# A hybrid decoder layer on one core: attention by pairs of heads over all tokens instead of by blocks of queries

## The chip, the cores and the metric

The kernel runs on one core of a Trainium2 chip. The metric is the device time of one execution in microseconds (us), the median of several runs; lower is better. The engines are TensorE (PE in the profile, with its weight loads as PEld), VectorE (DVE), ScalarE (ACT), GpSimd (POOL) and SyncE (SP, which here only issues DMAs). Each engine works through its own queue in order and waits on semaphores of the others.

## The reference

One layer over 512 tokens of width 1024, in float32: half a SwiGLU feed-forward (width 2816), a mixer, half a second feed-forward, each with an RMS norm before and after. The change is in the mixer alone.

```python
proj = h @ w_in          # 512 lru | 512 gate | 512 q | 128 k | 128 v
y_lru  = rg_lru(x_lru, ...) * gelu(gate_lru)
y_attn = sliding_window_sink_attention(q, k, v, sinks)   # 8 heads, 2 kv heads, dim 64
y = concat([rms_norm(y_lru, g_lru_out), rms_norm(y_attn, g_attn_out)]) @ w_o
# rg_lru: xc = conv4(x) + b;  r, i = sigmoid(block_diag(xc));  log_a = 8 r log_sigmoid(lam)
#         h_t = a h_(t-1) + sqrt(1 - a^2) i xc
# attention: a query sees itself and the 127 tokens before it, by blocks of 128:
#         p = exp(s - m) / (sum exp(s - m) + exp(sink - m));  out = p @ v
```

## The kernel before

Channels lie on partitions and the 512 tokens along the free axis, unless said otherwise. A product in full precision is three matmuls in rounded float32 (F32R): high by high, high by low and low by high (`mm3`); eight such steps of k make one product of 128 output channels. Splitting a tile into its parts is an ACT copy for the high part and a DVE subtraction for the low one. Matmuls on plain F32 tiles are used where no split exists, as in the values.

Weights pass through a class `Weights` (`W`): raw tiles of 1 MB loaded by SP into five buffers, each cut into units. `W.cast(n)` rounds the next units on ACT, `W.fill(n)` also subtracts on DVE and loads the next raw tile when one is used up, `W.take` hands a unit to PE. The order of all this is written out by hand: the program's order is each engine's queue.

The order in the mixer before:

- The boundary leaves the four lru input products (`xl_banks`) in PSUM. `conv_in` copies them to padded tiles on ACT, `conv` makes four taps (one on ACT, three on DVE).
- Products for k and v, then for the four q pairs. Product `pq{j}` holds head j of the first key-value head in rows 0 to 63 and head j of the second in rows 64 to 127. Between them `lru_gates` makes the two block-diagonal gates per 128 channels (PE, three ACT activations, one product on POOL).
- Then ten steps (`now`) over eight units (b, n): block b of 128 queries, key-value head n, four heads each. `scores` masks and takes the maximum on DVE, `exps` takes the exponential with its sum on ACT, `turn_p` transposes the four probability blocks on PE, copies them on ACT and masks them on POOL into a current and a previous part, `values` multiplies with the probabilities as stationary (128 columns) and v as moving (64 columns), and divides by the denominator at the end (`yn`). One unit is in `scores`, the one before in `turn_p`, the one before that in `values`. Block 0 uses unsplit copies (`q0`, `k0`).
- PE's filler is the four gate products (`fill_steps`, taken by `pump`, listed in `PUMPS`). The LRU's decay, root and scan and the gelu of the gates are put beside the steps by `later` and `run_due`.
- At the end the attention's rows lie with tokens on partitions and are transposed back (`atp`, 16 transposes) before they are split into high and low. `ssq` holds their sums of squares, from ACT.
- The output product `wo` takes attention channels first. After the first 36 matmuls `balance` makes the two norms, of which the LRU's comes from a PE product with a column of ones (`rms_lru`); `rescale` brings the attention half to the LRU's scale.

## Time and profile before

| | |
|---|---|
| median of 3 runs | 862.33 us (862.09 to 862.57) |
| profiled execution | 861.82 us, span 860.1 us |
| granted TensorE clock | 0.999 |
| PE busy | 850.4 us (99% of the span) |
| DVE, ACT, POOL busy | 647.5 (75%), 528.6 (61%), 168.0 us (20%) |

How to read it: the span goes from the first to the last instruction. A line of a group names the line of the kernel, the engine, the operation, the tiles (output, then inputs), the shape and the count, then the busy time in us and the mean of one in ns, then the idle time of the engine ahead of it and what ended it. In a timeline a line gives the start, the duration and the count of a run of like instructions; instructions of a full queue overlap slightly, so that a start minus the start before is less than a duration. A PE duration includes latency; what counts in a full queue is the distance between starts. In a table of stretches the numbers after the length are busy time (and count) of PE, PEld, DVE, ACT and POOL.

### The profile page before, as it was taken

The page shows a single profiled execution, that of the slowest core. Times are in us where ns is not written, and L with a number is a line of the kernel's source. Part 1 is how long each engine was busy: PE and PEld are TensorE (multiplying, and loading weights), DVE is VectorE, ACT ScalarE, POOL GpSimd, SP SyncE. Part 2 cuts the span into 40 slices and gives each one's busy share as a digit, 9 for nine tenths or more (in the row PEclk, how much of TensorE's full clock was granted, in tenths as well). Part 3 has the DMA queues.
Part 4 walks back from the last instruction along what each step waited for, and adds up shares of the span by engine and source line. Part 5 has one row for each costly group of instructions (what it writes and reads, how often), then busy time and mean ns, then how long its engine had stood idle before and what let it go on. Part 6 is the DMA issues. An engine that isn't in the chain of part 4 may idle for free.

```text
span 860.1 us, 14177 instructions
## 1 busy us (share of the span) xinstructions
PE 850.4 (99%) x5550; PEld 776.9 (90%) x5550; DVE 647.5 (75%) x883; ACT 528.6 (61%) x903; POOL 168.0 (20%) x202
## 2 busy tenths in 40 slices
PE   9999999999999999999999999999999999999996
PEld 8888999989989998998788889888998998998995
DVE  4989897887898866765688475357488788889856
ACT  6647567566576564755786677335556657658552
POOL 2022005014034011004255030001101402204402
PEclk9999999999999999999999999999999999999999
DMA  8265439739469463142112308235433945938912
GB/s 246 99 196 196 133 107 228 195 93 236 139 121 269 138 217 102 50 147 98 50 50 75 98 1 297 95 118 177 147 94 90 236 146 141 227 99 191 274 75 98
DMA packets 92867, 124.42 MB, mean 145 GB/s; under 512 B 5825, under 2 KB 62465, under 8 KB 92801
## 3 DMA queue, kind: packets, MB, share of 16 engines
q1 hardware_dynamic: 76240, 86.68, 31.8%
q0 software_dynamic: 16416, 36.71, 19.2%
q8 instruction: 43, 0.70, 0.3%
q14 instruction: 24, 0.19, 0.1%
q10 hardware_dynamic: 144, 0.13, 0.0%
HBM read 93.10 MB, written 30.41 MB: 144 GB/s over the span
## 4 chain that ended last, share of the span: by engine, by line
PE 93%; ACT 2%; DVE 2%; DMA 1%; POOL 1%; SPq 1%; issue 0%; DVEq 0%; ACTq 0%
PE aa L819 12%; PE ab L819 11%; PE da L819 6%; PE db L819 5%; PE wo L1624 4%; PE ba L819 3%; PE bb L819 3%; PE mn L701 1%; PE an L701 1%; PE yal L1146 1%; PE yal L1148 1%; PE yb L1148 1%; PE yb L1146 1%; PE yal L1147 1%; PE yb L1147 1%; PE yaa L1156 1%
## 5 line engine op out<-in xcount | busy, mean ns | idle before, releaser
L927 POOL DMA_DIRECT2D yp_a<-stage x42 | 37.0, 1160 | 146.4 <-ACT stage L924 141.2
L927 POOL DMA_DIRECT2D yp_b<-stage x42 | 36.5, 1121 | 149.0 <-ACT stage L924 142.8
L1175 POOL DMA_DIRECT2D yp_b<-stage x8 | 4.3, 541 | 91.8 <-ACT stage L1174 91.0
L1146 PE MATMUL yal<-whi_ad,hha 128*128 128x512 f32 x48 | 18.9, 393 | 0.0
L1148 PE MATMUL yal<-whi_ad,hla 128*128 128x512 f32 x48 | 18.7, 390 | 0.0
L1147 PE MATMUL yal<-wlo_ad,hha 128*128 128x512 f32 x48 | 18.7, 389 | 0.0
L1146 PE MATMUL yb<-whi_bd,hhb 128*128 128x512 f32 x48 | 18.7, 389 | 0.0
L1147 PE MATMUL yb<-wlo_bd,hhb 128*128 128x512 f32 x48 | 18.7, 389 | 0.0
L1148 PE MATMUL yb<-whi_bd,hlb 128*128 128x512 f32 x48 | 18.7, 389 | 0.0
L189 DVE TENSOR_TENSOR wlo_bd<-raw_bd,whi_bd 128x1024 fp32r<-128x1024 f32 x10 | 12.1, 1223 | 8.1 <-ACT whi_bd L184 8.1
L1297 POOL TENSOR_TENSOR xcl<-xc,xch 128x512 fp32r<-128x512 f32 x4 | 6.3, 1572 | 57.0 <-ACT xch L1296 57.0
L189 DVE TENSOR_TENSOR wlo_ad<-raw_ad,whi_ad 128x1024 fp32r<-128x1024 f32 x10 | 12.2, 1221 | 4.0 <-ACT whi_ad L184 4.0
L552 POOL TENSOR_TENSOR xg_f<-xh_f,xl_f 128x256 f32<-128x256 f32 x8 | 5.8, 767 | 43.9 <-DVE xl_f L483 43.9
L409 PE MATMUL gt<-xh_mx,whi_gt 128*128 128x512 f32 x32 | 14.2, 442 | 0.0
L602 ACT ACTIVATE sqxr<-x_rows 128x512 f32<-128x512 f32 x16 | 10.0, 631 | 5.6 <-DVE x_rows L632 5.6
L189 DVE TENSOR_TENSOR wlo_wo<-raw_wo,whi_wo 128x1024 fp32r<-128x1024 f32 x7 | 8.5, 1223 | 6.4 <-ACT whi_wo L184 6.2
L1147 PE MATMUL ybl<-wlo_bd,hhb 128*128 128x512 f32 (+1 forms) x36 | 13.2, 366 | 0.0
L1146 PE MATMUL ybl<-whi_bd,hhb 128*128 128x512 f32 (+1 forms) x36 | 13.2, 366 | 0.0
L1148 PE MATMUL ybl<-whi_bd,hlb 128*128 128x512 f32 (+1 forms) x36 | 13.2, 365 | 0.0
L1704 POOL TENSOR_TENSOR yp_b<-yp_b,grow 128x512 f32<-128x512 f32 x6 | 7.7, 1291 | 27.2 <-ACT ysq L1697 27.2
L1697 ACT ACTIVATE ysq<-yp_b 128x512 f32<-128x512 f32 (+1 forms) x9 | 5.2, 583 | 12.4 <-DVE yp_b L1696 11.7
L1624 PE MATMUL wo<-whi_wo,ylh 128*128 128x512 f32 x32 | 12.7, 396 | 0.0
(1841 smaller groups left out, 3719.9 us busy)
## 6 DMA issues: line engine op xcount, KB each, us to landing
yp_a<-stage POOLq DMA_DIRECT2D x50, 256.0 KB, 7.3
yp_b<-stage POOLq DMA_DIRECT2D x50, 256.0 KB, 7.8
raw_ad<-in_ffn_w_down SPq DMA_DIRECT2D x4, 1024.0 KB
raw_wo<-in_w_o SPq DMA_DIRECT2D x4, 1024.0 KB, 5.0
raw_bd<-in_ffn_w_down SPq DMA_DIRECT2D x4, 1024.0 KB
xn<-in_x SPq DMA_DIRECT2D x8, 256.0 KB, 3.0
x_rows<-in_x POOLq DMA_DIRECT2D x4, 512.0 KB, 12.4
yp_a<-yp_a POOLq DMA_DIRECT2D x8, 256.0 KB, 9.4
```

The costliest lines, as they stand in the source:

```text
L189: low.tensor_sub(two(lo, x), x, two(hi.bitcast(F32), x))
L409: pe.matmul(ps, hi[:, k, :], xh, start=start, stop=False)
L602: act.activation(wt(f"sq{name}{self.name}{tb}{dh}"), src, AF.Square, accum_out=self.ss[name, tb][:, dh:dh + 1])
L701: pe.matmul(b[:, l], w[part][:, k, :], xs[k][xpart][:, l], start=k + part + xpart == 0, stop=stop and k == KD - 1)
L819: pe.matmul(o, w[:, k, js], x, start=first and i + j + k == 0, stop=k == 3 and i == 2, skip_group_check=True)
L927: pool.dma_start(o, st.rearrange("p (a b) -> p a b", a=2) if len(o.shape) == 3 else st, accum_op=ALU.add)
L1146: pe.matmul(ps, hh[:, blk], hi[:, k, cs], start=start, stop=False)
L1147: pe.matmul(ps, hh[:, blk], lo[:, k, cs], start=False, stop=False)
L1148: pe.matmul(ps, hl_[:, blk], hi[:, k, cs], start=False, stop=stop)
L1156: pe.matmul(banks[i], hh[:, js], hi[:, k, :], start=first and k == 0, stop=False, skip_group_check=True)
L1624: pe.matmul(wo_banks[tb][dh], x, w[:, k, :], start=start and k == 0 and w is hi and not xp, stop=stop and k == 1 and xp == 1, skip_group_c ...
L1704: pool.tensor_mul(y, y, grow[dh][:, c0:c1])
```

## The change

Attention goes by pairs of heads j (head j of either key-value head) over all four query blocks.

- `products(j)` uses the split q and k for block 0 too and spreads the four blocks over two banks per head (block 1 and 2 in one, 0 and 3 with one key block less in the other).
- `scores(j, n)` has two more copies under the mask of 128 columns; the sink's exponential takes its bias on ACT.
- `normalise(j, n)`, new, adds the sink, takes the reciprocal and multiplies all four probability blocks on DVE, ahead of `turn_p`.
- `turn_p(j, n)` masks into tiles by key block (`pc`), with four smaller selects on POOL.
- `values(j)` has 64 columns of v as stationary and up to 256 columns of probabilities as moving; the two heads go to the two halves of the output partitions. The result has channels on partitions, so `yn` and the output transposes go. `rows_high` and `rows_low` split it and add up its squares (`acca`), whose mean is another PE product in `balance`.
- q products 1 to 3 and the gate products are the filler now, in the order q1, gt0, q2, q3, gt1 to gt3. The LRU's gates follow k, v and q0 directly; decay, root and scans 2, 3 stand ahead of pair 0's turn or behind it, scans 0 and 1 and the gelu steps in a table `beside`.
- `conv` reads the PSUM banks without padding; its split parts lie in other buffers. q3's low part is subtracted on DVE instead of POOL, and the deferred subtraction of one wo unit is gone. The wo rows of the attention half are loaded in two DMAs each, by channel order (d, j), and the gain row likewise.

```diff
+    def load_wo(k0, dh):
+        ...
+        for n in range(2):
+            sync.dma_start(raw[n * HD:(n + 1) * HD], src[n * KC * HD:(n + 1) * KC * HD].rearrange("(j d) c -> d j c", d=HD))
-    def conv(c0, xps):
+    def conv(c0):
+        for ci in (c0, c0 + 1):
+            act.activation(xcs[ci], xl_banks[ci], AF.Identity, bias=..., scale=...)
+        for back in range(1, CONV):
+            for ci in (c0, c0 + 1):
+                o = xcs[ci][:, back:]
+                dve.scalar_tensor_tensor(o, xl_banks[ci][:, :T - back], ..., o, op0=ALU.mult, op1=ALU.add)
+    def products(j):
+        ...
+        for b in range(NB):
+            i, o = ((1, 0), (0, 0), (0, 2 * P), (1, P))[b]
+            blk, keys = slice(b * P, (b + 1) * P), slice(max(b - 1, 0) * P, (b + 1) * P)
+            for p, (q_, k_) in enumerate(((qh, kh), (qh, kl), (ql, kh))):
+                for n, pr in enumerate(rows):
+                    pe.matmul(score_banks[j, n][i][:, o:o + keys.stop - keys.start], q_[pr, blk], k_[pr, keys], ...)
+    def scores(j, n):
+        ...
+        dve.copy_predicated(mid[:, 1::2, :], up8[:, :2, :], mid[:, 0::2, :])
+        dve.tensor_reduce(mx_[:, 1:3], mid[:, 1::2, :], op=ALU.max, axis=AX.X)
+        dve.copy_predicated(ends[:, 0, :], up8[:, 0, :], neg[:, :P])
+        dve.copy_predicated(ends[:, 2, :], up8[:, 0, :], ends[:, 1, :])
+        dve.tensor_reduce(mx_[:, 0::3], ends[:, 0::2, :], op=ALU.max, axis=AX.X)
+        dve.tensor_scalar(nm, mx_, -scale, nsink[:, h:h + 1], op0=ALU.mult, op1=ALU.min)
+    def normalise(j, n):
+        dve.tensor_add(den, den, es)
+        dve.reciprocal(den, den)
+        dve.tensor_mul(v4(sc), v4(sc), den.unsqueeze(2).to_broadcast([P, NB, P]))
+    def turn_p(j, n):
+        ...
+        act.copy(pa, pt)
+        for i, t in enumerate(pairs):
+            ...
+            pool.affine_select(t[:, :, 0, :], cur, ...)
+            pool.affine_select(t[:, :nb, 1, :], pre, ...)
+    def values(j):
+        o = bank(f"po{j}")
+        for b in range(NB):
+            w = P if b == NB - 1 else 2 * P
+            for n in range(2):
+                pe.matmul(o[n * HD:(n + 1) * HD, b * P:b * P + w], v[:, b * P + n * HD:b * P + (n + 1) * HD],
+                          unit[j, n][b // 2][:, 2 * (b % 2) * P:2 * (b % 2) * P + w], start=b == 0, stop=b == NB - 1, ...)
+    def rows_high(j):
+        x_high(ysp[KC + j], po[j], col("g_attn_out", j), ALL)
+        act.activation(acca, po[j], AF.Square)   # j > 0: a square of its own, added in rows_low
+    conv(0)
+    pk = in_product("pk", (), 1)
+    split_xc(0); split_xc(1)
+    W.cast(3)
+    conv(2)
+    W.fill(2)
+    kT = in_parts(pk, "kT")
+    split_xc(2); split_xc(3)
+    pv = in_product("pv", (), 2)
+    vT = taken(wt("vT"), pv)
+    lru_gates(0); lru_gates(1)
+    pq = in_product("pq0", (), 2)
+    lru_gates(2); lru_gates(3)
+    q_parts(0, pq)
+    ...                                   # v transposed back
+    pump(3)
+    products(0)
+    preload(AF.Exp)
+    ...                                   # decay_a 0-3, decay_b 0-3, preload(Sqrt), root 0-3
+    W.cast(2)
+    preload(AF.Exp)
+    for n in range(2):
+        scores(0, n); exps(0, n)
+    W.fill(2)
+    for n in range(2):
+        normalise(0, n)
+    pump(5)
+    for ci in range(KC):
+        root_u(ci)
+    SPLIT = W.taken + 3
+    beside = {0: [(scan, 0), (gelu_a, 0)], 1: [(scan, 1), (gelu_b, 0), (gelu_c, 0)], 2: [(gelu_d, 0)], 3: [(gelu_a, 1), (gelu_b, 1), (gelu_c, 1)]}
+    for j in range(KC):
+        if j:
+            values(j - 1)
+        for n in range(2):
+            if j:
+                scores(j, n); exps(j, n)
+        if j:
+            rows_high(j - 1)
+            W.fill(SPLIT + 2 * j - W.taken)
+        for n in range(2):
+            if j:
+                normalise(j, n)
+            else:
+                scan(2 + n)
+        if j == 0:
+            W.fill(SPLIT - W.taken)
+        W.cast(SPLIT + 2 * j + 1 - W.taken)
+        pump(5 if j else 8)
+        turn_p(j, 0)
+        pump(1)
+        turn_p(j, 1)
+        if j < KC - 1:
+            products(j + 1)
+        if j:
+            rows_low(j - 1)
+        W.fill(SPLIT + 2 * j + 1 - W.taken)
+        W.cast(SPLIT + 2 * j + 2 - W.taken)
+        for fn, i in beside[j]:
+            fn(i)
+        pump(4)
+    values(3)
+    ...
-    for ci, tp in enumerate(tps):
-        for b in range(NB):
-            pe.transpose(tp[:, b * P:(b + 1) * P], yns[b][:, ci * P:(ci + 1) * P], ident)
-        ...
-        ps = bank("rms_lru")
+        ps = bank("rms_mix")
+        for i, acc in enumerate((accl, acca)):
+            for b in range(NB):
+                pe.matmul(ps[:, i * NB + b:i * NB + b + 1], acc[:, b * P:(b + 1) * P], mean_c, start=True, stop=True)
```

386 lines of the change are left out of this document (140 added, 246 removed).

## The prediction

> **What bounds the kernel now.** I read the page's busy shares first, then a table of stretches, the chain that ended last, the timelines of the engines, and the groups by line with shapes kept apart.
>
> ```profile
> span 860.1 us, 14177 instructions
> PE 850.4 (99%) x5550; PEld 776.9 (90%) x5550; DVE 647.5 (75%) x883; ACT 528.6 (61%) x903; POOL 168.0 (20%) x202
> ...
> core 0: us, PE busy (x) PEld busy (x) DVE busy (x) ACT busy (x) POOL busy (x), PEclk, DMA share, GB/s
> 415.00:432.00 17.00, 16.94 (x115) 13.32 (x115) 13.01 (x27) 13.59 (x46) 6.58 (x9) 1.00 0.16 60
> 432.00:449.00 17.00, 17.00 (x139) 15.20 (x136) 14.48 (x33) 15.00 (x45) 7.64 (x12) 1.00 0.20 63
> 449.00:464.50 15.50, 15.23 (x101) 13.25 (x100) 13.70 (x19) 8.64 (x26) 13.55 (x14) 1.00 0.32 103
> ```
>
> TensorE (PE) is never idle for long, so a matmul taken away is worth its time as long as the others can follow. The mixer, which alone is changed, runs from 377.5 us (the key product) to about 464.6 us (the first output product). In the attention part (415 to 464.5) VectorE (DVE) is already busy 13.0, 14.5 and 13.7 us of 17, 17 and 15.5. That is 83%: there is little room behind PE.
>
> **The change on PE.** The chain that ended last, then PE's timeline, then groups and one line's instructions:
>
> ```profile
> 416.41 1.09 PE cur L1427 x16
> 427.49 0.84 PE po L1501 x8
> 431.74 1.63 PE sc L1438 x24
> 463.05 1.75 PE atp L1558 x16
> 464.80 8.18 PE wo L1624 x36
> 472.97 0.79 PE rms_lru L1601 x8
> ```
> ```profile
> 421.08 1.37 PE L1481 MATMUL pt<-ident,sc 128*128 128x128 f32 x4
> 426.19 0.60 PE L1481 MATMUL pt<-ident,sc 128*128 128x128 f32 x4
> 435.92 0.33 PE L1500 MATMUL po<-v,pp 128*128 128x64 f32 x2
> 437.62 0.48 PE L409 MATMUL gt<-xh_mx,whi_gt 128*128 128x512 f32 x1
> 453.23 0.98 PE L1481 MATMUL pt<-ident,sc 128*128 128x128 f32 x4
> 455.31 0.43 PE L1501 MATMUL po<-v,pa 128*128 128x64 f32 x2 [0.25 <-POOL pa L1488]
> ```
> ```profile
> L409 PE MATMUL gt<-xh_mx,whi_gt 128*128 128x512 f32 x32 | 14.2, 442 | 0.0
> L410 PE MATMUL gt<-xl_mx,whi_gt 128*128 128x512 f32 x32 | 12.5, 391 | 0.0
> L435 PE MATMUL an<-xl_mx,whi_xl 128*128 128x256 f32 x6 | 0.9, 283 | 0.0
> L469 PE MATMUL rms_x<-dg_x,ones x4: 377/378/379, 29.1 to 29.7; 128*128 128x256 f32 x4
> L1001 PE MATMUL warm<-ident 128*128 128x128 f32 x16 | 4.2, 441 | 1.4 <-POOL ident masks.py:199 1.4
> ```
>
> - *Values.* Before: two groups of 8 at 0.84, and six of 16 from 435.92 to 437.62, 1.70 each: 11.9 us. After, each pair needs per head 256+256+256+128 = 896 columns of plain f32. Plain f32 runs as two instructions (the spread of rms_x below is two products in the code, four in the row). From the durations, 391 against 283 ns says 0.42 ns a column for rounded operands plus some 0.17 us of latency; 378 ns at 256 columns says 0.81 for plain f32. So one head costs 2x896x0.81 = 1.45 us. If the two heads, in different column halves of the array, run side by side, a pair costs 1.45 plus some 0.3 for entry and exit, 1.75; one after the other 3.2. Four pairs: 7.0 or 12.8, that is -4.9 or +0.9. No row has column halves. The nearest, the row halves of the scores, overlap: 24 instructions of 256 columns in 1.63 us are 0.068 each, where one alone would need 0.107. I take -4.9.
> - By the Trainium skill (TensorE: Matmul & The Clock Gate, Part 3: Packing small matmuls) column groups run concurrently like row groups; by it this term would also be -4.9; no run shown here has it.
> - *Output transposes* go: -1.75.
> - *Scores.* One cur group (1.09) and three of 1.63 become four of 24, some smaller: +0.6.
> - *Statistic.* Sixteen one-column instructions for eight: +0.8.
> - *Returns to the products.* The first product after another kind is slower (442 against 391 ns over 32, some 0.085 for each of 20 returns by count in the timeline); about 14 remain: -0.5.
> - *PE's waits of today*: 1.37 and 0.98 against 0.60 for four transposes, and 0.25: 1.4 us. The places go: -1.4. Transposes of probabilities and values, gates and the ten input products stay in number.
>
> Sum if nothing waits anew: -4.9-1.75+0.6+0.8-0.5-1.4 = -7.2 us.
>
> **What the other queues must do.** Before, a unit's transposes came one step behind its scores, and its values two. After, one pair's scores, exponentials and division must all be through before PE may turn it (the division is now ahead of the transposes), and PE has only 56 product steps of 0.68 us (three at 0.2275, from 8.18 for 36) as filler, 16 of them ahead of the first turn.
>
> ```profile
> 375.90 2.36 DVE L189 TENSOR_TENSOR wlo_q<-raw_q,whi_q 128x1024 fp32r<-128x1024 f32 x2 [5.82 <-ACT whi_q L184]
> 397.26 0.69 DVE L1311 TENSOR_TENSOR qT0l<-pq,qT0h 128x512 fp32r<-128x512 f32 x1 [1.66 <-ACT qT0h L1310]
> 432.04 0.19 DVE L1505 RECIPROCAL rden<-den 128x8 f32<-128x8 f32 x1
> 432.33 0.69 DVE L1508 TENSOR_TENSOR yn<-po,rden 128x512 f32<-128x512 f32 x1
> 432.94 0.42 DVE L1454 COPY_PREDICATED sc<-up,sc 128x256 f32<-128x256 uint8 x1
> 433.39 0.42 DVE L1455 TENSOR_REDUCE mx<-sc 128x2 f32<-128x256 f32 x1
> ...
> 433.73 0.42 DVE L1454 COPY_PREDICATED sc<-up,sc 128x256 f32<-128x256 uint8 x1
> ...
> 434.65 0.16 DVE L1458 SCALAR_TENSOR_TENSOR nm<-mx,nsink 128x4 f32<-128x4 f32 x1
> ...
> 446.46 1.28 DVE L1404 TENSOR_TENSOR xc<-xc,th 128x512 f32<-128x512 f32 x2
> 447.66 2.73 DVE L1409 TENSOR_TENSOR_SCAN xc<-r,xc 128x512 f32<-128x512 f32 x2
> 455.49 1.59 DVE L1409 TENSOR_TENSOR_SCAN xc<-r,xc 128x512 f32<-128x512 f32 x1
> ```
> ```profile
> L1469 ACT ACTIVATE sc<-sc,nm 128x128 f32<-128x128 f32 x24 | 8.5, 371 | 0.4 <-DVE nm L1458 0.4
> L1469 ACT ACTIVATION_READ_ACCUMULATOR sc<-sc,nm 128x1 f32 x24 | 5.0, 210 | 0.0
> L387 ACT ACT_TABLE_LOAD x3 | 3.8, 1283 | 0.1
> L1393 ACT ACTIVATE r<-r,ka 128x512 f32<-128x512 f32 x4 | 3.0, 739 | 0.0
> L1395 POOL TENSOR_TENSOR m<-r 128x512 f32<-128x512 f32 x4 | 4.2, 1039 | 1.0 <-ACT r L1393 1.0
> L1488 POOL TENSOR_SCALAR_AFFINE_SELECT pa<-pa 128x512 f32<-128x512 f32 x8 | 7.3, 909 | 2.3 <-ACT pa L1483 1.9
> ```
>
> In a full queue an instruction costs its duration less about 0.08 (two scans 2.73, next at +2.64), and 0.03 more than its duration where it needs the one before.
>
> *Front (to the first turn).* Products pk and pv (48 by 0.2275) end at 388.4, as today. Two gates (12, to 391.1), pq0 (24) and two more gates follow. The low part of pq0's weights now stands on DVE behind the six taps of conv(2) and its two casts on ACT; by those queues PE waits some 0.5, and the gates end at 399.8. ACT then has six activations (0.64 each) done at 402.0. qT0's high and low part take to 403.3, where PE, after the transposes of v and three steps, asks for them at 402.3 (scores of pair 0): 0.8. ACT runs a table load with its dummy (1.3), four decays (2.6, from 403.8 to 406.3); POOL's four squares at 1.04 end at 408.7, DVE's last sum and the last root at 410.2, a cast (1.0) and a table load take to 412.3, four exponentials with their reads (0.345 the pair, and es) to 414.0, and the division (0.16+0.19+0.69 with steps, 1.02) to 415.1. PE, with products(0) and 13 steps from 403.1, is there at 413.9: 1.2, and some 0.5 at the next two places. Front: 3.0 us. It is bounded by 0 (every low part early) and by 4.5 (this chain of 12 us a tenth longer). What pays for it is the LRU work taken ahead, which before lay beside the first steps and was not waited for.
>
> *Pair 0 to pair 1.* DVE's queue from the last exponential of pair 0 (415.6) to the end of the first division of pair 1: two divisions 2.04, qT1 low 0.61, two u products 1.20, two scans 2.64, a third 1.5, three weight splits (q3, gt1, gt2; 2.36 for two) 3.45, the copy of gate 0 0.60, scores of pair 1 twice (0.45+0.34+0.20+0.31+0.45+0.12, the 128-column copies taken as 0.28) 3.74: 15.8 us, ready at 431.4. PE in that stretch: turn 0.4, products(1) 1.75, nine steps with returns 6.3, values(0) 1.75, from 416.8: 427.0. PE waits 4.4 us at the turn of pair 1, and everything behind it on PE with it. DVE is late here, not ACT: exponentials of a head group take 1.6 us, DVE's scores of one 1.87.
>
> *Later rounds.* q2's two parts stand behind the exponentials, two activations on po, a cast on ACT and the divisions on DVE, so products(2) waits about 1.5, products(3) 1.4 in the same way. Otherwise pair 1 to pair 2 is 12.8 us on DVE (two divisions 2.04, 1.3 of waiting for that cast of q2, two low parts 1.27, two splits 2.3, a scan 1.5, a gelu step 0.64, scores 3.74) and as much on PE (two turns, ten steps 7.1, the 1.5, products and values 3.5), and pair 2 to 3 is 11.9 against 12.7. POOL's 32 smaller selects have as many elements as today's 14 (7168 a partition); a pair's eight, 1792, are 3.5 of today's at 0.909, 3.2 us, and fit into the 5.5 us of steps and products before its values; if not, up to 0.5 a pair. At the end the statistic of the LRU half must be ready 36 output products (8.18) after the last gate product, where today the output transposes stand between as well (9.9); but the high and low parts of three pairs have left ACT's and DVE's queues by then (three by 0.69 on each), so I cost it at nothing, with 1 us if that is not enough. The wo load in halves adds two issues on SP, whose queue is otherwise as long as before; a raw tile comes free when q3 is split, some 10 us ahead of the cast: nothing, and 1 us if it queues. q3's split moves from POOL to DVE and is counted above. conv reads PSUM, so four ACT copies and the memsets go, off the path; the gain row by 64 channels is loaded at the start, long before its use: nothing.
>
> New waits: 3.0+4.4+1.5+1.4 = 10.3. Net -7.2+10.3 = +3.1. Walking the queues in order instead of adding gives +2.4 at the first wo product of the last token block, since some waits take in others; applied to the kernel before, the same walk ends 0.7 late. I take +2.5. The profiled run took 861.82 us (span 860.1, 1.7 around it), 0.5 below the median of 862.33: on the median, 864.8. A change under 0.2% (1.7 us) can't be told from none.
>
> **Rivals.**
> 1. *DVE keeps up* (faster). If DVE's 15.8 us between pair 0 and pair 1 were 11.4, the 4.4 would go and the 1.5 shrink with it, and about -2.8 be left: 859.5. For it: rows vary (one scan advances the queue by 1.32, another by 1.51). Against: nearly all of the 15.8 are rows above, and the sum breaks even only with 2.5 us less.
> 2. *Column halves run in turn* (slower). +5.8 on PE; two of the four pairs hide in waits, +2.9 to 3: 867.7. For it: no row shows halves by columns in plain f32.
> 3. *A cold clock* (slower). The first TensorE instructions of the trace, of 128 plain columns, took 441 ns, where 256 such columns take 378 later; if a 4 us gap brings that state back for a time like the opening's (12 of them at twice the step of 0.107, 2.6 us instead of 1.3), 1.3 to 3 us are added: 866.8. Against: the granted clock is 1.00 in every stretch, but no gap before is over 1.4 us. The Trainium skill (TensorE: Matmul & The Clock Gate, Why this matters for your kernels) says that a gap over some 3 us sends the clock to half; this trace has no such gap.
>
> **How the numbers follow.** My case 0.50 (its own range 862.8 to 867, of which 0.2 lies within 0.2%), rival 1 0.25, rival 2 0.13, rival 3 0.12. Slower 0.55, within 0.2% 0.20, faster 0.25. The range goes from deep in rival 1 (858.0) to rival 2 with more contention (869.0).
>
> **What will show it.** A wait of PE on DVE of some 4 us ahead of the second pair's transposes, with DVE busy nearly without gaps for the 16 us before; waits of 1 to 1.5 at the scores of pairs 2 and 3; values of a pair in 1.75 us (3.2 means rival 2); the granted clock after the gap (rival 3). Wrong if DVE has gaps in that stretch, or if the front's 3 us are not there.

## The result, and the profile after

The changed kernel takes 871.52 us (median of 4 runs, 869.65 to 871.97); the kernel before, run beside it, takes 862.21 us. The ratio is 1.0103 with a 95% interval from 1.0086 to 1.0121: slower by 9.3 us. The prediction said slower, but 864.8 us and at most 869.0. The profiled execution of the changed kernel was the quickest of its four, 869.65 us; its span is 7.8 us longer than that of the kernel before (860.1).

The page's busy shares, and then the waits of TensorE (PE): us in total, how often, the longest.

```profile
span 867.9 us, 14095 instructions
PE 847.4 (98%) x5502; PEld 768.3 (89%) x5502; DVE 657.3 (76%) x898; ACT 527.4 (61%) x896; POOL 173.9 (20%) x211
```
```profile
PE pt L1376 <- DVE den L1366: 6.8, 3, 4.8
PE warm L1002 <- POOL ident masks.py:199: 1.4, 1, 1.4
PE rms_mix L1579 <- DVE acc_lru L1555: 1.0, 1, 1.0
PE po L1394 <- POOL pc L1386: 0.9, 1, 0.9
...
PE pt L1376 <- ACT yah L481: 0.3, 1, 0.3
PE sc L1340 <- DVE qT2l L1316: 0.3, 1, 0.3
...
PE sc L1340 <- ACT qT2h L1315: 0.2, 1, 0.2
...
```

Apart from the warm-up (1.4, there before as well) all that is shown lies in the mixer, and they are the loss: some 10.1 us of waiting between 376 and 500 us where the kernel before had 0.25. A table of stretches shows the engines in the three stretches that the prediction quoted of before, in the longest gap, and in the 16 us behind it:

```profile
core 0: us, PE busy (x) PEld busy (x) DVE busy (x) ACT busy (x) POOL busy (x), PEclk, DMA share, GB/s
415.00:432.00 17.00, 13.48 (x78) 10.20 (x78) 16.55 (x31) 9.43 (x32) 7.45 (x8) 0.90 0.40 81
432.00:449.00 17.00, 14.22 (x95) 10.47 (x93) 14.24 (x32) 12.36 (x39) 5.05 (x8) 1.00 0.43 106
449.00:464.50 15.50, 14.92 (x92) 10.97 (x90) 14.25 (x29) 9.67 (x28) 7.63 (x14) 1.00 0.25 78
412.80:417.60 4.80, 0.00 (x0) 0.03 (x1) 4.52 (x14) 4.79 (x22) 0.00 (x0) 1.00 0.01 2
417.60:433.60 16.00, 13.83 (x78) 10.17 (x78) 15.62 (x28) 8.43 (x26) 7.45 (x8) 0.89 0.52 105
```

PE was busy in 16.94 of the first 17 us before and is now busy in 13.48; DVE went from 13.01 to 16.55. The granted clock, 1.00 in every stretch before, is 0.90 there. PE's timeline has the places:

```profile
417.60 0.72 PE L1376 MATMUL pt<-ident,sc 128*128 128x128 f32 x4 [4.80 <-DVE den L1366]
427.00 1.73 PE L1394 MATMUL po<-pc,v 128*64 128x256 f32 x14 [0.92 <-POOL pc L1386]
433.71 0.63 PE L1376 MATMUL pt<-ident,sc 128*128 128x128 f32 x4 [1.35 <-DVE den L1366]
440.75 1.73 PE L1394 MATMUL po<-pc,v 128*64 128x256 f32 x16
442.42 0.50 PE L410 MATMUL pq<-xh_mx,whi_q 128*128 128x512 f32 x1
470.06 0.39 PE L1602 MATMUL wo<-whi_wo,yah 128*128 128x512 f32 x1
479.33 1.05 PE L1579 MATMUL rms_mix<-mean_c,acc_lru 128*128 128x1 f32 x8 [0.95 <-DVE acc_lru L1555]
```

The first output product starts at 470.06 (464.56 before, +5.5 us); the wait for the statistic and its eight further instructions add 2.0 more. A pair's values, from 440.75 to the next product at 442.42, take 1.67 us, where the prediction had 1.75 for column halves side by side and 3.2 for one after the other: they do run side by side.

Where did the 7.8 us come from? Taking each row's start to the next row's start from 376 to 500 us, the waits rise by 9.9 us, and the work on PE that the change touches falls by 2.1 (at full clock by 3.9, in a later kernel without the slow rows); 9.9 - 2.1 = 7.8.

### The profile page after: what moved, and what is told of

It is laid out like the page before. It is cut to its first block, busy times and chain, and to the rows that moved or that the text cites. A ratio compares the mean times of both kernels' runs of the same rounds, so it can differ in the third digit from the quotient of the medians.

```text
span 867.9 us, 14095 instructions
## 1 busy us (share of the span) xinstructions
PE 847.4 (98%) x5502; PEld 768.3 (89%) x5502; DVE 657.3 (76%) x898; ACT 527.4 (61%) x896; POOL 173.9 (20%) x211
## 4 chain that ended last, share of the span: by engine, by line
PE 85%; DVE 7%; ACT 4%; DMA 2%; issue 1%; SPq 0%; POOL 0%; DVEq 0%; ACTq 0%
PE aa L820 12%; PE ab L820 11%; PE da L820 6%; PE db L820 5%; PE ba L820 3%; PE wo L1602 3%; PE bb L820 3%; PE an L702 1%; PE mn L702 1%; PE yal L1148 1%; PE yal L1149 1%; PE yal L1147 1%; PE yb L1149 1%; PE yb L1147 1%; PE yb L1148 1%; DMA raw_second<-in_ffn_w_gu 1%
## 5 line engine op out<-in xcount | busy, mean ns | idle before, releaser
L1385 POOL TENSOR_SCALAR_AFFINE_SELECT pc<-pa 128x256 f32<-128x256 f32 x16 | 10.8, 676 | 32.3 <-ACT pa L1378 32.3
L1268 DVE SCALAR_TENSOR_TENSOR xc<-an,cols,xc 128x511 f32<-128x511 f32 (+2 forms) x12 | 8.2, 742 | 9.0 <-ACT xc L1264 9.0
L410 PE MATMUL pq<-xh_mx,whi_q 128*128 128x512 f32 x32 | 13.6, 425 | 0.0
```

The source lines that it names most:

```text
L410: pe.matmul(ps, hi[:, k, :], xh, start=start, stop=False)
L1268: dve.scalar_tensor_tensor(o, xl_banks[ci][:, :T - back], col("conv_w", (CONV - 1 - back) * KC + ci), o, op0=ALU.mult, op1=ALU.add)
L1385: pool.affine_select(t[:, :, 0, :], cur, pattern=[[0, 2], [1, P]], base=0, channel_multiplier=-1, compare_op=ALU.is_ge, fill=0.0)
```

## The experiments

Theory at the start: the recurrence's decays, ahead of pair 0's exponentials and stretched because DVE and POOL work on SBUF at once, make the 4.8 us gap, and the gap makes half a clock behind it. Rival: DVE owes too much between 403 and 465 us, wherever one puts it. The edits are shortened: `...`, and words such as `x4` or `scores, exps of pair 0`, stand for code that isn't shown. Profiled runs reach the mixer up to 1.3 us apart, by what happens ahead of it; where that matters, times are counted from the key product. DVE's and POOL's timelines of the changed kernel, on which the theory rests:

```profile
404.79 6.12 DVE L1301 SCALAR_TENSOR_TENSOR th<-m,th 128x512 f32<-128x512 f32 x4 [1.96 <-POOL m L1298]
...
420.19 2.70 DVE L1310 TENSOR_TENSOR_SCAN xc<-r,xc 128x512 f32<-128x512 f32 x2
422.82 1.35 DVE L177 TENSOR_TENSOR wlo_q<-raw_q,whi_q 128x1024 fp32r<-128x1024 f32 x1
424.10 1.30 DVE L177 TENSOR_TENSOR wlo_gt<-raw_gt__4213,whi_gt 128x1024 fp32r<-128x1024 f32 x1
```
```profile
403.71 4.94 POOL L1298 TENSOR_TENSOR m<-r 128x512 f32<-128x512 f32 x4 [1.85 <-ACT r L1296]
...
420.50 1.32 POOL L1386 TENSOR_SCALAR_AFFINE_SELECT pc<-pa 128x256 f32<-128x256 f32 x1
421.77 1.32 POOL L1385 TENSOR_SCALAR_AFFINE_SELECT pc<-pa 128x256 f32<-128x256 f32 x1
423.05 1.28 POOL L1386 TENSOR_SCALAR_AFFINE_SELECT pc<-pa 128x128 f32<-128x128 f32 x1
424.29 1.38 POOL L1385 TENSOR_SCALAR_AFFINE_SELECT pc<-pa 128x256 f32<-128x256 f32 x1
...
426.91 0.40 POOL L1385 TENSOR_SCALAR_AFFINE_SELECT pc<-pa 128x256 f32<-128x256 f32 x1
```

Beside scans and weight splits each select takes as long as one DVE instruction, 1.3 us, whatever its size; beside a copy out of PSUM it takes 0.40. The Trainium skill (SBUF — State Buffer, Who interferes with whom) says that a DVE instruction with two SBUF inputs contends with a GpSimd instruction that reads SBUF, and that the ports they share are an exclusive lock; these rows agree.

### First four: the front

**Squares of the decays on ACT.**

```diff
-        pool.tensor_mul(m, a, a)
+        act.activation(m, a, AF.Square)
```

> The four squares of the decays go from POOL (4.94 us for four) to ACT. Theory (the chain of the recurrence, stretched by DVE and POOL working on SBUF at once, holds up pair 0's exponentials): the four sums on DVE fall from 6.1 us to about 3.2, the roots on ACT end about 2 us earlier, the PE gap ahead of the first turn falls from 4.8 to about 2.8, and the time by 2 to 2.5 us, to about 869. Rival A (the stretch of DVE is not POOL's doing): the sums stay near 6 us, the time stays at 871.5. Rival B (DVE's queue is the limit): the front gains 2 us and the wait at the turn of pair 1 (1.35 us) grows by as much; the time stays within 0.5 us.

872.54 us (869.43 to 873.18). The stretch was POOL's doing, since each of the four sums now takes 0.69 us; the first:

```profile
404.55 0.69 DVE L1301 SCALAR_TENSOR_TENSOR th<-m,th 128x512 f32<-128x512 f32 x1 [1.50 <-ACT m L1298]
```

But the gap is still 4.4 us. ACT, on which the rest of that chain runs, has four more activations, and the last root ends at 412.0 instead of 411.6. The wait changed its name, not its length. None of the three came: not the theory's gap of 2.8, not rival A's sums of 6 us, and not rival B's longer wait at the turn of pair 1 (1.00 us, 1.35 in the changed kernel). What the sums gained was lost to ACT in the front itself, not to DVE behind it.

**Pair 0 first.**

```diff
     preload(AF.Exp)
+    scores, exps, normalise of pair 0; W.cast(2); W.fill(2); pump(5)
     for ci in range(KC): decay_a(ci)
     ...
-    scores, exps, W.fill(2), normalise of pair 0; pump(5)
     for ci in range(KC): root_u(ci)
```

> The part 'lru chain ahead' alone is undone: scores, exponentials and division of pair 0 come first, then the decays, sums and roots; as many table loads as before. Theory (the chain ahead makes the 4.8 us gap and the half clock behind it): the gap falls under 1 us, the granted clock stays full, the time falls by about 6 us, to about 865.5. Rival (DVE's backlog): what DVE owes only moves; the wait at the turn of pair 1 grows from 1.35 to over 4 us and the time falls by no more than 2.5 us, to about 869.

871.87 us. The gap ahead of the turn went, and a larger one came at the values of pair 0:

```profile
PE po L1394 <- POOL pc L1386: 8.2, 2, 7.0
```

It was ACT's queue: the copies of pair 0's turned probabilities stand behind the roots (which wait for the stretched sums, the last until 419.48), a table load and two casts, and run at 423.41, 9 us after the second transposes began (414.57). POOL, whose products with the roots were done at 420.58, idled 3.5 us for these copies. Neither expectation came true: no gain, and no wait at all at the turn of pair 1, where the rival had over 4 us.

**Extra matmuls in the gap.**

```diff
+        if (j, n) == (0, 0):
+            for _ in range(20):
+                pe.matmul(pt, kT[0][:, :P], kT[0], start=True, stop=True)
```

> Twenty extra matmuls of 128x512 (about 0.22 us each) stand ahead of the first turn and fill the 4.8 us gap; their result is overwritten. Theory (the half clock after the gap costs about 1.8 us): the transposes start when they did, the granted clock stays at 1.0, and the time falls by 1.5 to 2 us, to about 869.7. Rival (the slow rows right behind the gap are hidden by the next wait, on the turn of pair 1): the wait there grows by as much and the time stays within 0.4 us of 871.5.

871.54 us (869.94 to 873.13): the clock stays at 1.00 there, and what PE gains it waits for inside the values of pair 0, which go on at 427.48 (427.00 in the changed kernel). The rival was right, but with another wait than the one it named:

```profile
PE po L1397 <- POOL pc L1389: 2.5, 1, 2.5
```

**The weight split behind pair 0's division.**

```diff
-    W.fill(2)
     for n in range(2):
         normalise(0, n)
+    W.fill(2)
```

> The weight split on DVE (1.22 us) that stands ahead of pair 0's division moves behind it. Theory (the division waits for the split, not for its exponentials alone): the division of the first head starts about 0.8 us earlier, the gap falls from 4.8 to about 4.0, the time by about 0.7 us. Rival (the exponentials set it): gap and time stay within 0.3 us.

872.35 us (871.0 to 874.61): the gap fell to 4.08, and PE waited 0.68 for the split weights right behind and 1.6 at the turn of pair 1. The gap did as expected, the time didn't. Each of the four took something off the 4.8 us and gave it back by the turn of pair 1.

### The statistic and the slow rows behind it

Three of the four profiles have something else that the profile of the changed kernel doesn't have. In the one with squares on ACT, PE's clock is at half from 480.7 to 487.5 us:

```profile
478.00:480.00 2.00, 1.03 (x8) 0.61 (x6) 1.35 (x2) 1.97 (x4) 0.00 (x0) 1.00 0.00 0
480.00:482.00 2.00, 2.00 (x15) 2.00 (x14) 1.66 (x3) 2.00 (x4) 0.00 (x0) 0.68 0.00 0
482.00:484.00 2.00, 2.00 (x5) 1.61 (x6) 1.97 (x6) 1.38 (x4) 0.00 (x0) 0.50 0.00 0
484.00:486.00 2.00, 2.00 (x6) 1.52 (x6) 1.71 (x2) 0.00 (x0) 0.00 (x0) 0.50 0.02 4
486.00:488.00 2.00, 2.00 (x7) 1.55 (x6) 0.00 (x0) 0.01 (x1) 0.00 (x0) 0.61 0.00 0
```

Only 0.97 us of waiting stands ahead of it, and then 2 us of 16 one-column matmuls.

```diff
+            if (n, xp) == (2, 0):
+                balance()
+                W.fill(4)
         if n == 1:
             ...
-            balance()
-            W.fill(4)
```

> The statistic's 16 one-column matmuls move behind the next 12 matmuls of the output product (2.7 us). Theory (the 0.95 us wait for the LRU branch's sum, and the little that PE does in the 2 us behind it, set off a half clock of up to 6.8 us in part of the runs): the wait goes, no slow rows between 478 and 490 us in any run, 0.9 us less in the best run and 2.5 us less in the median (about 869.0), and the runs lie closer together. Rival (the wait is only 0.95 us and the slow rows come all the same from the one-column matmuls): 0.9 less, with the same spread.

868.83 us (868.76 to 869.24): 2.7 below the changed kernel, and the runs lie within 0.5 us where they lay 2.3 apart. The statistic runs from 481.31 to 483.01 without a wait, and the slow rows are gone:

```profile
482.00:484.00 2.00, 2.00 (x15) 1.85 (x15) 1.60 (x5) 1.15 (x4) 0.00 (x0) 1.00 0.00 0
484.00:486.00 2.00, 2.00 (x10) 1.62 (x9) 2.00 (x3) 0.56 (x1) 0.00 (x0) 1.00 0.00 0
```

The changed kernel's quickest run, 869.65, had no slow rows, and less the wait it would be 868.7; so 0.95 us of the 2.7 is the wait, and the rest, by this reckoning, the half clock in the other runs, which have no trace. The Trainium skill (TensorE: Matmul & The Clock Gate, Why this matters for your kernels) warns of idle gaps above some 3 us; the 4.80 us gap agrees, and the 0.97 us one, with one-column matmuls behind it, shows that a shorter one can do it too. The length alone doesn't decide it. Behind waits of 0.95 to 0.97 us at the statistic the half clock lasted 0 us (the changed kernel, the late weight split), 3.4 us (pair 0 first, extra matmuls) or 6.8 us (squares on ACT); in kernels below, 3.4 us behind a wait of 0.48, and 3.4 and 10.2 us behind two of 3.2. No profile without a wait there has any.

### The chain of the recurrence elsewhere

**All of it behind pair 0's turn.**

```diff
-    decays, sums, roots, root products ahead of pair 0; scan(2), scan(3) in round 0
+    beside = {0: [decay_a x4, decay_b x4, ...], 1: [root_u x4, ...], 2: [scan 0, scan 1, ...], ...}
+    preload(Sqrt); root x4; preload(Exp) behind exps(1); scan(2), scan(3) behind rows_low(3)
```

> The whole recurrence chain goes behind pair 0's turn: decays and sums beside round 0, roots behind pair 1's exponentials, products with the roots beside round 1, scans 0 and 1 beside round 2, scans 2 and 3 behind the last values. (In the earlier kernel with pair 0 first, the decays' squares and root products still stood ahead of pair 0's selects on POOL, and the 7 us wait moved to the values.) Theory (between 403 and 434 us DVE owes the chain's 11 us, pair 0's and pair 1's work at once, and POOL's selects are held up beside it; the chain in that place is the cost): no PE gap over 1 us up to the turn of pair 1, no half clock there, and about 6 us less: 865.5. Rival (DVE's total is the limit, wherever the chain stands): the waits reappear at the turns of pairs 1 to 3 and the time falls by less than 2 us.

881.23 us, the worst of all. PE waits 5.9 us at the turn of pair 1, 3.9 at the scores of pair 2, 3.2 at the statistic:

```profile
PE pt L1376 <- DVE den L1366: 7.6, 3, 5.9
PE sc L1340 <- ACT qT2h L1315: 3.9, 1, 3.9
PE rms_mix L1574 <- DVE acc_lru L1550: 3.2, 1, 3.2
```

Between 415 and 420 us DVE is busy 1.39 us of 5: its sums stand ahead of pair 1's scores and wait for squares that POOL takes up only behind the selects, at 417.88. My theory fell with this: it isn't enough to take the chain away from the front. With the statistic moved as well:

```diff
+            if (n, xp) == (2, 0):
+                balance()
```

> Both edits: the chain behind pair 0 and the statistic later. Theory: the two savings add, about 6 + 2.5 us: 863, within 1.5 us of before. If PE's own work has shrunk by the 4 to 7 us that the prediction counted and every wait goes: below 862, so faster than before. Rival (DVE's total): not below 867.

875.41 us: the statistic's wait falls from 3.2 to 0.5 and saves 5.8 us together with most of its slow rows (half clock for 3.4 us instead of 10.2), but the rest stays, as the rival said.

**The scans alone.**

```diff
-            else:
-                scan(2 + n)                      # round 0
-    beside = {0: [(scan, 0), ...], 1: [(scan, 1), ...], ...
+    beside = {0: [...], 1: [(scan, 0), ...], 2: [(scan, 1), ...], ...
     rows_low(3)
+    scan(2); scan(3)
```

> Only the scans move: 2 and 3 (2.7 us on DVE in round 0) behind the last values, 0 and 1 one round later each. Theory: the gap ahead of the first turn stays 4.4 to 4.8 us, the selects of pair 0 meet less DVE work, the waits at values 0 (0.92) and at the turn of pair 1 (1.35) go: 2 to 2.5 us less, about 869. Rival (selects and ACT, not DVE's queue, set round 0): within 0.6 us of 871.5.

871.8 us, no gain, but for a reason that one can see: the waits at the values of pair 0 and at the turn of pair 1 went, the turn of pair 3 came at 456.81 instead of 459.47, and then the sum of the LRU branch was late.

```profile
PE rms_mix L1579 <- DVE acc_lru L1555: 3.2, 1, 3.2
```

So scans 2 and 3 went ahead of `rows_low(3)`, and the statistic to its later place:

```diff
+    scan(2); scan(3)
     rows_low(3)
-    scan(2); scan(3)
...
+            if (n, xp) == (2, 0):
+                balance()
```

> The scans moved as in the earlier kernel (0 and 1 a round later), but 2 and 3 stand ahead of the last pair's low parts on DVE, where it idled 3 us; the statistic stands behind 12 more matmuls. The gap ahead of the first turn (4.8) and its half clock are left as they are. Theory (round 0's wait is DVE's scans and weight splits beside POOL's selects; the end lost what that gained to the wait for the LRU branch's sum): turn 3 comes about 2.7 us earlier than in the changed kernel and the end keeps it: 2.5 to 3 us below the kernel with the statistic alone moved, about 866. Rival (whatever leaves round 0 is owed again by DVE ahead of the sum): the statistic waits 2 us or more and the time is 868.5 or above.

866.67 us (866.54 to 867.01), near what was expected: another 2.2 us below the kernel with the statistic alone (2.5 to 3 expected). This kernel answers the question of the slow clock in the front too. Again with the twenty matmuls:

```diff
+            for _ in range(20):
+                pe.matmul(pt, kT[0][:, :P], kT[0], start=True, stop=True)
```

> The kernel with late scans and late statistic (866.67), with the twenty extra matmuls in the 4.8 us gap. Nothing behind that gap waits for POOL any more. If the half clock (about 5 us long at 0.5) delays PE there: 1.5 to 2.5 us less, about 864.7. If what PE gains is waited for again at the values of pair 0 or the turn of pair 1: within 0.5 us of 866.7.

867.47 us (867.05 to 867.78). The clock, and nothing else, improved; first the kernel without the matmuls, then with them:

```profile
418.00:423.00 5.00, 5.00 (x31) 4.28 (x31) 5.00 (x7) 3.66 (x5) 2.80 (x3) 0.50 0.01 3
```
```profile
418.00:423.00 5.00, 4.74 (x42) 3.73 (x41) 4.93 (x9) 4.60 (x8) 1.77 (x3) 1.00 0.01 3
```

In both DVE is busy in practically all of the 5 us. Five us at half the clock cost nothing there, because PE was going to wait for DVE anyway: with the matmuls it reaches the turn of pair 1 earlier and waits 0.47 us there, 0.5 at products(2) and 0.67 at the turn of pair 2, where the two kernels are level (65.83 us behind the key product without them, 65.79 with them). From the key product to the last output product it is 138.71 us without and 138.65 with them. In the profiled run with them the key product came 1.04 us later, behind half a clock from 9.4 to 12.8 us, 400 us ahead of the gap; that is about the difference of the two profiled runs (867.78 and 866.8).

### DVE's total

**The chain in pieces.** Pair 0 first; the decays' exponentials behind it under the same table; sums behind the division; roots behind pair 0's turn; the root products all on POOL behind the selects; scans and statistic as above.

```diff
+    scores, exps of pair 0; decay_a x4; normalise of pair 0; W.cast(2); W.fill(2); decay_b x4; pump(5)
...
+        if j == 0: preload(Sqrt); root x4; preload(Exp)      # behind products(1)
+        if j == 1: root_u(0..2)                              # behind values(0)
-        (pool if ci < 2 else dve).tensor_mul(us_[ci], us_[ci], th[ci])
+        pool.tensor_mul(us_[ci], us_[ci], th[ci])
```

> As the one before, and the front in another order: pair 0's scores and exponentials first, the decays' exponentials behind them under the same table, the sums behind the division on DVE, the roots behind pair 0's turn where ACT idled 5.3 us, and the products with the roots all on POOL where it idled 8.6 us; nothing waits for POOL ahead of the selects. Theory (the order of the queues around pair 0 is the cost, PE's own work has shrunk): no gap over 1 us ahead of turn 0, turn 1 near 426 instead of 433.7, full clock throughout, and a time of 860 to 863, the same as before or below. Rival (DVE owes the same total, its queue holds the turns of pairs 1 to 3 by 2 us each): 866 or above.

867.45 us, as the rival said. No gap at the turn of pair 0, but 3.2 us at products(1), where q1's low part stood behind the sums on DVE, and 2.3 us at the turn of pair 3, both with half clock beside them. Put right, with the squares of decays 2 and 3 on DVE:

```diff
+    scores, exps of pair 0; decay_a(0), (1); W.cast(2); normalise; W.fill(2); pump(5); decay_a(2), (3); decay_b x4
-        pool.tensor_mul(m, a, a)
+        (pool if ci < 2 else dve).tensor_mul(m, a, a)
```

> The kernel with the chain split up, with two of its queues put right: q1's low part (68-ns-per-100-columns work of 0.68 us that products 1 waited 3.18 us for) now stands ahead of the decays' sums on DVE, the weight cast ahead of half of the decays' exponentials on ACT, and the squares of decays 2 and 3 (0.65 us each by the row of a 128x512 product) on DVE, so that POOL is free for the selects about 3 us earlier. Theory (each wait behind pair 0 was one instruction queued behind another engine's late work): no wait over 1 us and full clock up to the turn of pair 2: 3 to 5 us below the kernel before it, 862.5 to 864.5. Rival (DVE's total, 95% of every stretch from 415 to 465 us, is the limit): the gain of the front comes back as waits at the turns of pairs 2 and 3 and the time is 866 or above.

866.38 us, 0.3 below the kernel that left the 4.8 us gap alone: the turn of pair 2 came at 443.18 there and at 443.26 in that one. Counted from the key product that is 64.75 and 65.83 us, so that of a gap of 4.8 us only 1.1 was left by then: PE waited 1.6 us inside the values of pair 0 and 2.5 at the turn of pair 1 instead. That points to a bound further back, as the rival had it: DVE, which is 91 to 92% busy in the stretches from 415 to 464.5 (not 95% as I had written; nor is 0.68 us for 512 columns 68 ns per 100, but 133). The gate copies on ACT:

```diff
-        gts[ci] = taken(wt(f"gt{ci}"), b)
+        gts[ci] = wt(f"gt{ci}")
+        act.copy(gts[ci], b)
```

> The same, and the four copies of the gate products out of PSUM (0.66 to 0.68 us each) go from DVE to ACT, which has idle time in every round (60% busy). If DVE's total is the limit: 0.7 us less for each of the first two copies that lie ahead of the last turn, 1 to 1.5 us below the kernel before it. If the queues' order is: within 0.4 us of it.

866.32 us, by the time alone the case of the queues' order. But the turns of pairs 2 and 3 came 1.7 us earlier (1.1 us counted from the key product), and the last values then waited 0.56 and 1.36 us (0.89 in the kernel before), the second time for selects that scans 2 and 3 held up. Two tests on this kernel. First the three masked copies of each head's scores left out:

```diff
-        dve.copy_predicated(mid[:, 1::2, :], ...)
-        dve.copy_predicated(ends[:, 0, :], ...)
-        dve.copy_predicated(ends[:, 2, :], ...)
```

> The same kernel (866.3, its scans left where they are) with the three masked copies of each head's scores left out, so that maxima and sums run over unmasked columns (24 copies, about 1.0 us of DVE a head, 8 in all). If DVE's total is what holds the turns of pairs 1 to 3: they come about 2 us earlier each up to the waits that are there (1.3, 0.7, 0.9 and some 0.5 at the low parts of q), 2.5 to 3.5 us less in all: about 863. If the selects on POOL and the order of the queues hold them: at most 1 us less, 865.3 or above.

860.79 us (860.49 to 861.17): 5.5 us less for about 8 us of DVE's work, with every select left. DVE's work holds the rounds, by more than I had expected. Whether as a total, or because these copies stand between a pair's scores and its turn, this run alone doesn't tell; but the scans and the gate copies don't stand there, and the turns moved with them too (2.7 us earlier at pair 3 for two scans of 2.7 us together, and 1.1 us for two copies). PE in the 55 us from 410 to 465, first with the copies, then without:

```profile
410.00:465.00 55.00, 47.51 (x292) 34.73 (x291) 47.44 (x87) 39.69 (x101) 31.41 (x39) 1.00 0.31 82
```
```profile
410.00:465.00 55.00, 52.15 (x315) 39.23 (x314) 45.61 (x70) 40.61 (x103) 34.11 (x41) 1.00 0.35 91
```

Then scans 2 and 3 behind `rows_low(3)`, the statistic six matmuls later still:

```diff
-    scan(2); scan(3)
     rows_low(3)
+    scan(2); scan(3)
...
-            if (n, xp) == (2, 0):
+            if (n, xp) == (2, 1):
```

> The last kernel (chain split up, gate copies on ACT, 866.3) with scans 2 and 3 behind the last pair's low part instead of ahead of it, where they stretched POOL's last selects and PE waited 0.56 and 1.36 us inside the values; the statistic goes 6 matmuls (1.4 us) later still, to make room for the later sum. Theory (POOL's selects, each held for the length of a DVE instruction, set the last values): 1.5 to 2 us less, about 864.5. Rival (DVE owes the scans anyway): the wait moves to the statistic, within 0.5 us of 866.3.

864.78 us (864.47 to 865.11), 1.5 less, as expected. Then work out of that stretch rather than within it, the split of q2's and q3's weights ahead of the last gates:

```diff
-    pq = in_product("pq0", (), 2)
+    pq = in_product("pq0", (), 4)
```

> The kernel with the scans last (864.78), and the casts and low parts of q2's and q3's weights (2 on ACT by 1.05, 2 on DVE by 1.22) move ahead of the last gates, where ACT idled 3.5 us and DVE 6.3. Theory (DVE's total between 410 and 465 us holds PE): the turns of pairs 1 and 2 come 1.5 to 2.5 us earlier and the time is about 862.8, near the kernel before. Rival (selects or ACT hold pair 1): within 0.6 us of 864.8.

862.75 us (862.38 to 863.3; the kernel before beside it 862.27): 2.0 less, the loss gone. The casts on ACT moved along, so the 2.0 us need not be DVE's alone. DVE's work in the idle stretch ahead, first the kernel with scans earlier and gate copies on ACT, then this one:

```profile
390.00:403.00 13.00, 12.91 (x65) 10.36 (x65) 4.03 (x5) 9.51 (x15) 7.26 (x5) 1.00 0.25 82
```
```profile
390.00:403.00 13.00, 12.90 (x66) 10.40 (x66) 6.29 (x7) 12.35 (x18) 7.04 (x5) 1.00 0.54 148
```

Carrying three more splits out at the other end went wrong:

```diff
-            W.fill(SPLIT + 2 * j - W.taken)
+            W.fill(SPLIT + j - W.taken)
...
-        W.cast(SPLIT + 2 * j + 2 - W.taken)
+        W.cast(SPLIT + j + 1 - W.taken)
```

> The same, and the weights are split one a round instead of two, so that three splits (3.7 us of DVE, 3.2 of ACT) move from rounds 1 to 3 to the output products behind 467 us, where DVE was busy 3.6 of 5 us. Theory (DVE's total in the rounds): the last turn comes 2 to 3 us earlier again, the output products wait up to 1 us for their weights; about 861, the same as before or faster. Rival (the output products wait for the late splits as long as the rounds gained): 862.5 or above.

877.73 us. The rounds gained 0.7 us counted from the key product (turn of pair 3 at 451.96, 453.07 before), but the cast of the first output weights came late and PE stood:

```profile
PE wo L1610 <- ACT whi_wo L172: 11.4, 1, 11.4
```

Last, the order on ACT in each round:

```diff
-        W.cast(SPLIT + 2 * j + 1 - W.taken)
         pump(5 if j else 8)
+        W.cast(SPLIT + 2 * j + 1 - W.taken)
```

> The last kernel (862.75), and on ACT the weight cast of a round (1.05 to 1.09 us) goes behind the rounding of q2 and q3 instead of ahead of it. If ACT's order holds the low parts of q on DVE, and DVE's total then holds the turns: the waits at products 2 and 3 go (0.9 and 0.5 us), DVE's idle 1.1 to 1.4 us in each of the two rounds goes, and the time falls by 1 to 2 us, to about 861.3, below the kernel before. Rival (copies of the turned probabilities and the selects become late by the cast, or the turns wait as before): within 0.5 us of 862.75.

861.34 us (860.7 to 861.42; before 862.24), ratio 0.9990, interval 0.9981 to 0.9999: as expected, and just below the kernel before, by less than the 0.2% that I called measurable. The waits for q's parts are gone, and 51.87 us of PE's 55 are busy (45.81 in the changed kernel, 54.67 before). This one took nothing off DVE: in the same 55 us DVE is busier than in the kernel before it (47.76, 45.87 there), since it no longer stands still behind ACT.

```profile
410.00:465.00 55.00, 51.87 (x313) 38.78 (x312) 47.76 (x87) 38.35 (x100) 29.97 (x40) 1.00 0.30 85
```
```profile
PE pt L1376 <- DVE sc L1368: 1.1, 1, 1.1
PE po L1394 <- POOL pc L1386: 1.0, 3, 0.5
PE pt L1376 <- ACT yah L481: 0.9, 1, 0.9
```

## Why the prediction was wrong

Right were the sign, its reason (DVE can't keep up with pairs whose division stands ahead of the turn), the sum of the new waits (10.3 added up, 9.7 after the walk; 10.1 measured; but with the places wrong, as told below, this was luck), and the column halves (1.75 predicted, 1.67 measured, rival 2 is out). Rival 1, that DVE keeps up, is out: with DVE's work as the change placed it, it didn't.

Three steps failed: the sum on PE, with the values as its largest part; the wait of the front; and the clock, which had been left to a rival of small chance. In the prediction's own terms, from +2.5 to the measured +7.8 of the span:

- *The sum on PE, -7.2.* Start to start, and at full clock (the last kernel), the places that the change touches gave -3.9, and the 0.25 us wait of before -0.25 more: -4.1, so 3.1 us less gain. Values 12.43 to 8.57 us (-3.9, not -4.9: a pair that runs through takes 1.67, better than predicted, but three of the four stop in the middle for a select on POOL, and such a pair takes 2.30 without the wait itself; in the same way pair 0 of the changed kernel takes 2.31); scores 5.97 to 6.88 (+0.9, not +0.6); the returns to the products gained nothing (input and gate products together 45.88 to 46.24, +0.4 where I took -0.5); the turns 3.98 to 3.45 (-0.5, where I had taken the stretched ones at -1.15). Output transposes (-1.7) and statistic (+0.9) were right to 0.1.
- *The waits: right sum, wrong places.* The front was 1.2 at the first turn in the prediction and 4.80 in the trace. Of these 3.6 us, 1.1 is PE, which came to the place at 412.8 and not at 413.9. The rest is the chain that the division waits for, which ended at 417.45 and not at 415.1. Its largest part is the four sums on DVE, which I took one by one behind POOL's squares at the earlier rows; they took 6.12 us, and 0.69 each once POOL was away, so that the last root ended at 411.6 and not at 410.2: 1.4. Another 0.7 is the weight split on DVE ahead of the division (1.22 us, from 415.23), which my chain leaves out; moved behind, it shortened the gap by 0.7. Since PE came late to everything behind, the wait at the turn of pair 1 was 1.35 and not 4.4, and 0.5 each at products 2 and 3, not 1.5 and 1.4. I had costed the selects by their elements, 3.2 us a pair and nothing on PE, with 0.5 kept; pair 0's eight took 7.4 us (420.11 to 427.55), each held by one DVE instruction, and PE waited 0.92. The 1 us kept for the statistic was 0.95, though I had costed it at nothing.
- *Rival 3, the cold clock, 0.12.* It came, in two places. In the front it added 1.8 us to PE's rows in the profiled run (3.9 - 2.1), but not to the time: kept warm, the kernel is no faster. Behind the statistic, where I hadn't looked at all, it is the likely reason that the runs lie from 869.65 to 871.97, and taking the place away gave 2.7 us with its wait.

Adding these: 3.1 (PE's sum) + 0.4 (waits, 10.1 for 9.7) + 1.8 (slow rows in the front) are the 5.3 us by which the profiled run lies above the prediction's net; the median lies 1.9 above the profiled run, where I had put 0.5. That makes the 6.7 us from 864.8 to 871.5. The cause is another matter than the sum: where DVE holds PE, a slow clock cost nothing by itself, and a smaller gain on PE should not have either, though no run shows that. From the changed kernel to the last one, 10.2 us: 2.7 for the statistic's place; 2.2 for scans out of round 0; 0.3 for the order of the front; 0.1 for the gate copies; 1.5 for the last scans away from the last selects; 2.0 for two weight splits carried ahead; 1.4 for one cast behind q. The four large ones are DVE's work placed elsewhere, or the statistic; the 1.4 is ACT's order, on which DVE waited. What I should have asked of my walk is not where PE waits first but how much DVE owes in all ahead of each turn in the 55 us from 410 to 465, and what POOL does beside it. First before, then after:

```profile
410.00:465.00 55.00, 54.67 (x375) 46.36 (x374) 43.01 (x79) 40.10 (x120) 29.56 (x34) 1.00 0.21 68
```
```profile
410.00:465.00 55.00, 45.81 (x276) 33.89 (x276) 50.30 (x101) 35.49 (x105) 22.68 (x33) 0.97 0.34 82
```

DVE went from 43.01 to 50.30 us of the 55. The busy time alone doesn't decide it: with the gate copies on ACT, DVE was busy 47.44 us and PE 47.51, in the last experiment 47.76 and 51.87. It is the work that stands ahead of the turns that counts.

Open: how much of PE idling, and for how long, brings the half clock behind the statistic (0 to 6.8 us of it behind nearly the same wait in five kernels), since no run varied the length alone, or took the one-column matmuls away; how far DVE holds the rounds by its total and how far by its order, since every edit that moved work also changed the order; and whether the returns to the products cost what I took them for, since no run took them apart.

## What to carry to other kernels

Where an engine off the path is over nine tenths busy in a stretch, add up its whole debt there before you look at single waits: taking one wait away then only moves it, and carrying two weight splits out of the stretch was worth more than removing a gap of 4.8 us. Before you move a step in an in-order queue, ask what waits behind it when it waits: roots on ACT ahead of the copies of the turned probabilities cost 7 us, sums on DVE ahead of the scores 6. A small wait next to many one-column matmuls deserves a look at the clock, and at the spread of the runs.

## What the runs showed of the hardware

- Half the clock for up to 6.8 us behind a wait of 0.97 us and 16 one-column matmuls, not in each profile (0, 0, 3.4, 3.4 and 6.8 us in five kernels with waits of 0.95 to 0.97).
- Half the clock for 5 us without a measurable cost, where PE was about to wait (138.71 us from the key product to the last output product with it, 138.65 without).
- Two matmul streams in two column halves, in plain f32, side by side: 1.67 us a pair when it runs through, 2.30 us and the wait when it stops in the middle.
- A select of 128x256 on POOL takes 0.40 us, and 1.3 us beside DVE work on two SBUF inputs; one of 128x128 took 0.29 and 1.28. The number of selects counts then, not their elements.
- Sums of 128x512 on DVE: 0.69 us each with POOL idle, 6.12 for four with POOL's products beside them.
